# A hybrid conformer and stick-breaking layer: meta scores with the meta keys as the stationary operand, and later, spaced steps for values that are turned and packed

## The chip, the cores and the metric

The kernel runs on one core of a Trainium2 chip. The metric is the device time of one execution in microseconds (us). The engines are TensorE (PE in the profile, with PEld its weight loads), VectorE (DVE), ScalarE (ACT), GpSimd (POOL) and SyncE (SP), which issues DMAs.

## What is computed

One layer over 2048 frames of 1024 channels, with 16 learned meta tokens put ahead of them. All of it is float32.

```python
def hybrid_layer(h, ...):
    u = rms_norm(h, pre_g)
    glu_a, glu_b, conv_gate, q, k, v, sb_gate = split(u @ w_in)      # 7 x 512 columns
    c = causal_depthwise_conv(glu_a * sigmoid(glu_b), conv_w, conv_b)  # width 31
    c = silu(layer_norm(c)) @ w_pw2 + b_pw2
    c = c * silu(conv_gate)
    s = stick_breaking_attention(q, k, v) * silu(sb_gate)            # 8 heads x 64
    return h + rms_norm(concat([c, s]) @ w_out, post_g)

# stick breaking, per head, strictly causal (s < t):
#   z = q.k / 8,  A[t,s] = sigmoid(z[t,s]) * prod over s<j<t of (1 - sigmoid(z[t,j])),  out = A @ v
```

## The kernel before

The frames are worked in four chunks of 512 (`TC`), numbered c = 0 to 3; channels lie on the 128 partitions. A float32 product is made of three products of a high and a low part (`hi`, `lo`, of type fp32r): high by high, high by low, low by high. The projections (`proj`, rows `mm<-uh,w` and `mm<-ul,w`) do so over eight blocks of the contraction; a 128-column block of weights is the stationary operand and 512 frames stream past it.

Attention (`attention`) takes a head and a chunk of keys at a time, in four blocks of 128 queries. `weigh` makes scores into a PSUM bank (`T<-kk,q`), ScalarE takes 1 - sigmoid in place, VectorE's scan multiplies these up from the newest key back (`pr`). `flip` transposes the running products (`T<-ident,pr`) and splits them into `ah` and `al`; `gather` multiplies with the values (`av<-ah,vk`). The running products telescope, so `gather` uses differences of neighbouring values: `differences` makes them on GpSimd (`ev`), and `turn` transposes them by four on TensorE (`T<-ident,ev`), splits them and stores them. `short` lets `gather` go ahead of `weigh` at the last block of a diagonal chunk.

The 16 meta tokens are keys for every query. Their scores are made apart, by `meta_scores`, called for each of the four head pairs j of a chunk 3 us after the pair's query projection: for each block of 128 frames the queries are the stationary operand and the meta keys `km` (32 columns of two heads, high and low) stream past. VectorE adds the two halves into `sgm`, frames on partitions; there are two such tiles, for even and odd chunks, and the second lies in the tile `cp`, so its rows in the profile are named `cp`. When a chunk's attention is done, `meta_keys` turns these scores into weights (a sigmoid, four scans, a copy `bm` on GpSimd), transposes them by four into one PSUM bank, and for each head pair splits 32 rows of that bank into high and low (`mixs<-T,mixs 32x512`) and packs them, high, low and high again, into 96 rows. One product with packed values `vm` (`T<-mixs,vm`) gives the meta tokens' part, to which VectorE adds the attention's sum `sr` and then multiplies with the gate `gt`. The results of all four pairs (`mixs`) are what the output projection `out_proj` of that chunk waits for.

PSUM has eight banks: two for `mm`, four for `T`, one each for `av` and `cv`. `T` banks are taken in a ring: the fourth allocation after one gets the same bank again. The scores of attention, the transposes, the meta scores and the packed products all take `T` banks.

The order of instructions on each engine is set when the program is built. Generators yield the time from which their next piece could run; `merge` chooses between three streams (the attention as main, projections and output as fill, `meta_keys` as extra) by a planner's clock, which has its own costs for each engine's operations (`pe_cost` and others) and corner points (`SHARES`) for how far the fill may be ahead. `when` queues a later step with the tiles it reads and writes. On the chip each engine runs its list in order. All instructions are recorded in one helper, so the profile gives them all line 218; they are told apart by their tiles.

Of the kernel before, what the change touches and what calls it, by code (L numbers as in the profile page):

```python
# [11 lines left out]
F32 = mybir.dt.float32  # L12
F32R = mybir.dt.float32r
# [6 lines left out]
P = 128  # L20
# [3 lines left out]
NM = 16  # L24
# [32 lines left out]
def slab_keys():  # L57
# [17 lines left out]
BEFORE = 0, 2, 0, 0  # L75

SHARES = (
    [(28.1, 169.2)], [(71.5, 214.4)], [(114.3, 214.4)], [(123.8, 97.4), (158.7, 126.3)],
)


# [56 lines left out]
class Later:  # L138
# [1 line left out]

    count = 0

    def __init__(self, clock, what, ins, outs, engine, date, room):
        self.clock, self.what, self.ins, self.outs = clock, what, ins, outs
        self.engine, self.date, self.room = engine, date, room
# [16 lines left out]
    def at(self):  # L162
        t = max([self.date] + [self.clock.at(a, self.n) for a in self.ins])
        if self.room:
            t = max(t, self.clock.next_free(self.room))
        return t


class Engine:
# [51 lines left out]


def pe_cost(name, n, kw):
    return (0.108 if name == "transpose" else max(n * 4.537e-4, 0.06)), 0.19


def dve_cost(name, n, kw):
# [39 lines left out]
def trunk(ctx: ExitStack, tc: tile.TileContext, x, xturn, xlater, meta, cpack, post_g, wpack, out):  # L267
# [13 lines left out]
        while clock.writers(mark):  # L281
            run(clock.writers(mark)[0])

    def when(what, ins, outs=(), engine=None, date=0.0, tag=None):
        soon.append(Later(clock, what, ins, outs, engine, date, tag))

    pe = Engine(clock, nc.tensor, pe_cost, 0.15, run)
    dve = Engine(clock, nc.vector, dve_cost, 0.04, run)
# [42 lines left out]
    def need(*aps, tag=None, given=None, evs=0, n=1):  # L331
# [20 lines left out]
    both = const.tile([P, ncp + NTB * NH * MS], F32, name="cp")  # L352
    cp = both[:, : ncp + KD * NM]
    cw = cp[:, 0 : NJ * CW].rearrange("p (j w) -> p j w", w=CW)
    o = NJ * CW
    preg = cp[:, o : o + KD]
# [26 lines left out]

    vm = const.tile([P, NJ, P], F32R, name="vm")
    vl = const.tile([P, 2, P], F32R, name="vl")
    km = const.tile([P, 2, NJ, 2 * NM], F32R, name="km")
    cm = const.tile([P, NTB, NH, MS], F32, name="cm")
    sgm = [
        const.tile([P, NTB, NH, MS], F32, name="sgm"),
        both[:, ncp:].rearrange("p (b h s) -> p b h s", b=NTB, h=NH),  # L390
    ]
    ct = [const.tile([P, HIST + TC], F32, name=f"ct{j}") for j in range(NJ)]

    def clear():
        for j in range(NJ):
            nc.gpsimd.memset(ct[j][:, 0 : HIST - NM], 0.0)
        nc.gpsimd.memset(km.bitcast(F32), 0.0)
        nc.gpsimd.memset(vm.bitcast(F32), 0.0)
        nc.gpsimd.memset(vl.bitcast(F32), 0.0)
        nc.gpsimd.memset(cm, 0.0)  # L400

    kscr = dr.tile([NH, 2, HD, NM + SEQ], F32, name="kscr")
    qscr = dr.tile([NJ, 2, P, NM + SEQ], F32, name="qscr")
# [494 lines left out]
    def qk_proj(c, g, scr, with_meta):  # L898
        for j in range(NJ):
            o0 = 0 if (with_meta and c == 0) else NM  # L900
            hilo = []

            def ev_qk(pt, o, n):
                if not hilo:
                    hilo.extend(T("ehl", [P, NM + TC], EHL, F32R) for _ in range(2))
                hi, lo = hilo
                act.activation(hi[:, o : o + n], pt, AF.Copy)
                dve.tensor_tensor(
                    lo[:, o : o + n], pt, hi[:, o : o + n].bitcast(F32), op=ALU.subtract
                )  # L910

            yield from proj(c, g + j, ev_qk, with_meta)
            hi, lo = hilo

            def store(j=j, hi=hi, lo=lo):
                cols = slice(c * TC + o0, (c + 1) * TC + NM)
                for i, t in ((0, hi), (1, lo)):
                    if g == G_Q:
                        sp.dma_start(scr[j, i, :, cols], t[:, o0:].bitcast(F32))
                        continue  # L920
                    for e in range(2):
                        sp.dma_start(
                            scr[2 * j + e, i, :, cols],
                            t[e * HD : (e + 1) * HD, o0:].bitcast(F32),
                        )
                if g == G_Q and j == 0:
                    keep["q", c] = True
                    in_us(4.5, lambda: load_first(c))

            when(store, [hi, lo], ["q" if g == G_Q else "k"])  # L930
            if g == G_Q:
                when(
                    lambda a=(c, j, hi, lo): meta_scores(*a), [hi, lo], [sgm[c % 2]], tag="T",
                    date=pe.now + 3.0,
                )

    def meta_scores(c, j, hi, lo):

        sg = sgm[c % 2]
        if j == 0:  # L940
            pool.memset(sg[:, :, :, NM:], 0.0)
        pt = PT("T", [P, TC])[:, : NTB * 4 * NM].rearrange("p (b i s) -> p b i s", b=NTB, i=2)
        for r in range(NTB):
            ts = slice(NM + r * P, NM + (r + 1) * P)
            pe.matmul(pt[:, r], hi[:, ts], km[:, :, j, :], start=(r == 0), stop=False)
            pe.matmul(
                pt[:, r, 0], lo[:, ts], km[:, 0, j, :], start=False, stop=(r == NTB - 1)
            )
        a, b = (pt[:, :, i].rearrange("p b (e s) -> p b e s", e=2) for i in range(2))
        dve.tensor_copy(sg[:, :, 2 * j : 2 * j + 2, 0:NM], b)  # L950
        dve.tensor_tensor(
            sg[:, :, 2 * j : 2 * j + 2, 0:NM], a, sg[:, :, 2 * j : 2 * j + 2, 0:NM], op=ALU.add
        )
        if j == NJ - 1:
            keep["sgm", c] = True

    def in_proj(c):
        yield from pairs(c, range(BEFORE[c], NJ))
# [51 lines left out]
    def values(c):  # L1010
# [3 lines left out]
        for j in range(NJ):  # L1014
# [16 lines left out]
            def differences(vt, j):  # L1031
                o = 0 if c == 0 else NM
                dv = T("ev", [P, 1 + NM + TC], EV)[:, : NM + TC]
                pool.tensor_tensor(
                    dv[:, o:], vt[:, o : NM + TC], vt[:, o + 1 :], op=ALU.subtract
                )
                pool.tensor_copy(vcol[c % 2][:, j], vt[:, NM + P :: P])
                when(lambda: turn(dv, j, P, NM, NTB), [dv], [f"v{j}"], tag="T")
                if c == 0:
                    when(lambda: turn(dv, j, NM, 0, 1), [dv], [f"v{j}"], tag="T")  # L1040

            def turn(dv, j, rows, t0, nb):
                pt = PT("T", [P, NTB, P])[:rows, :nb]
# [26 lines left out]
    def meta_k():  # L1070
        force("k")
        for e in range(2):
            rows = slice(e * HD, (e + 1) * HD)
            for i in range(2):
                sp.dma_start(
                    km[rows, i, :, e * NM : (e + 1) * NM].bitcast(F32),
                    kscr[e::2, i, :, 0:NM].rearrange("j d s -> d j s"),
                )

# [205 lines left out]
    def attention(c, mixs):  # L1285
# [15 lines left out]
        def weigh(u, r):  # L1301
# [22 lines left out]
            u["a"].append(pr)  # L1324
            if kc == 0 and c == NCH - 1 and h >= EARLY:
                bm = keep["bm"][:, h - EARLY, r, h]
                zm = sgm[c % 2][:, r, h, 0:NM]
# [113 lines left out]
        for i in range(len(order) + 1):  # L1441
# [8 lines left out]
                    if 0 < kc == c and h + 1 < NH:  # L1450
                        heads[h + 1] = load_q(c, h + 1)
            for b in range(NTB if u else len(flips)):
                ready = len(pend) >= LAG
                short = ready and pend[0][0]["diag"] and pend[0][1] == NTB - 1
                for what in (1, 0) if short else (0, 1):
                    if what == 0 and u:
                        yield need(heads[u["h"]]["q2"], u["kk"], tag="T")
                        weigh(u, b)
                    if what and ready:
                        yield needs_of(*pend[0])  # L1460
                        gather(*pend.pop(0))
# [41 lines left out]
    def meta_keys(c, h0, h1, mixs):  # L1503
# [10 lines left out]
        hold.add(bm.name)  # L1514
        if part:
            pool.memset(bm, 0.0)
        sg = sgm[c % 2]
        zm = sg[:, :, hs, 0:NM]
        act.activation(zm, zm, AF.Sigmoid, scale=-SCALE)
        for r in range(NTB):  # L1520
            fl = lambda t: t[:, r, hs].rearrange("p h s -> p (h s)")[:, ::-1]
            dve.tensor_tensor_scan(
                fl(sg), fl(sg), fl(cm), 0.0, op0=ALU.mult, op1=ALU.max
            )
        when(lambda: pool.tensor_copy(bm[:, :, hs], zm), [sg], [bm])
        given = {}
        force("s")
        force("g")
# [42 lines left out]
        for j in js:  # L1571
# [347 lines left out]
    def last_room(c):  # L1919
# [8 lines left out]
        zm = sgm[c % 2][:, :, EARLY:, 0:NM]  # L1928
        act.activation(zm, zm, AF.Sigmoid, scale=-SCALE)
        keep["pg"] = a[:, 2:4]  # L1930
        sp.dma_start(
# [109 lines left out]
```

## Time and profile before

| | |
|---|---|
| median of 3 runs | 1317.13 us (1316.32 to 1318.55) |
| the profiled execution | 1318.35 us, its span 1316.6 us |
| TensorE busy | 1292.9 us (98%), 7522 matmuls |
| VectorE busy | 1023.1 us (78%) |
| ScalarE busy | 734.8 us (56%) |
| GpSimd busy | 674.9 us (51%) |
| DMA | 300.82 MB, 228 GB/s on average |

A row of the timeline has the start in us from the span's start, the busy time, the engine, the line, the operation with what it writes and reads, the number of instructions merged and, in brackets, how long the engine stood idle before and who released it. A row of groups has the count, the busy time in us, the mean of one in ns, and the idle time before with its releasers. A row of waits has the total in us, how many times, and the longest. A row of stretches has the length, the busy time of PE, PEld, DVE, ACT and POOL with the number of instructions, the granted TensorE clock as a share of full speed, the DMA share and GB/s. The ends of matmuls are modelled, so the rows of matmuls overlap; their starts are recorded.

### The profile page before, as it was taken

What the parts mean: (1) busy time and instruction counts of PE and PEld (TensorE: products, weight loads), DVE (VectorE), ACT (ScalarE), POOL (GpSimd) and SP (SyncE); (2) the same over time, 40 slices, a digit from 0 to 9 for tenths busy, and PEclk for the clock granted to TensorE, in tenths of its full rate; (3) what the DMA queues carried; (4) which work ended last, traced back from release to release, by engine and by line L of the source; (5) the groups of instructions that cost most, each with busy time, mean ns of one, the idle gap of its engine ahead of it and who ended that gap; (6) DMA issues with size and microseconds to landing.
All of it is one profiled execution on the core that took longest, in us unless ns stands there. A gap on an engine that the chain in (4) does not pass through costs nothing.

```text
span 1316.6 us, 22042 instructions
## 1 busy us (share of the span) xinstructions
PE 1292.9 (98%) x7522; PEld 1115.8 (85%) x7522; DVE 1023.1 (78%) x1470; ACT 734.8 (56%) x1461; POOL 674.9 (51%) x807
## 2 busy tenths in 40 slices
PE   8999999999999999999999999999999999999897
PEld 8998888887799878887789988888787889888797
DVE  5999889998884588984587478985448987899964
ACT  6544355344465452676555544588775665666543
POOL 2555578767677430788742231499787212322402
PEclk9999999999999999999999999999999999999999
DMA  6687787999878996676756696666667456676555
GB/s 230 217 266 234 240 274 258 304 342 321 267 241 269 314 299 196 204 233 215 229 180 193 188 342 198 195 193 215 200 185 231 137 156 191 193 250 217 177 160 184
DMA packets 166399, 300.82 MB, mean 228 GB/s; under 512 B 17280, under 2 KB 71744, under 8 KB 166288
## 3 DMA queue, kind: packets, MB, share of 16 engines
q1 hardware_dynamic: 152496, 251.44, 61.5%
q0 software_dynamic: 13792, 47.98, 9.5%
q8 instruction: 59, 0.97, 0.3%
q14 instruction: 52, 0.43, 0.1%
HBM read 221.90 MB, written 77.46 MB: 227 GB/s over the span
## 4 chain that ended last, share of the span: by engine, by line
PE 86%; DVE 6%; DMA 3%; ACT 2%; issue 1%; POOL 1%; SPq 0%; DVEq 0%; POOLq 0%; ACTq 0%
PE mm L218 56%; PE T L218 21%; PE av L218 9%; DVE pr L218 1%; DMA w<-wscr 1%; DMA ev<-x 1%; DVE ul L218 1%; DVE tok L218 1%; DVE cv L218 1%; DMA tok<-xlater 1%; POOL ev L218 1%; DVE mixs L218 1%; DMA pr<-xturn 0%; DVE al L218 0%; PE cv L218 0%
## 5 line engine op out<-in xcount | busy, mean ns | idle before, releaser
L218 PE MATMUL mm<-uh,w 128*128 128x512 f32 (+1 forms) x1936 | 566.9, 379 | 1.8 <-ACT uh L218 1.5
L218 PEld LDWEIGHTS mm<-uh,w 128*128 128x128 f32 x1936 | 338.7, 190 | 54.2 <-ACT uh L218 2.2
L218 PE MATMUL mm<-ul,w 128*128 128x512 f32 (+1 forms) x968 | 358.9, 372 | 0.0
L218 DVE TENSOR_TENSOR_SCAN pr<-T,pr,zcol 128x512 f32<-128x512 f32 x192 | 245.2, 1277 | 56.6 <-ACT T L218 54.0
L218 DVE TENSOR_TENSOR al<-T,ah 128x512 fp32r<-128x512 f32 (+1 forms) x320 | 191.3, 598 | 102.9 <-ACT ah L218 101.4
L218 ACT ACTIVATE ah<-T 128x512 fp32r<-128x512 f32 (+1 forms) x320 | 170.1, 532 | 156.1 <-PE T L218 155.0
L218 DVE SCALAR_TENSOR_TENSOR cv<-ct,cp,cv 128x512 f32<-128x512 f32 x319 | 238.9, 749 | 6.7
L218 ACT ACTIVATE T<-T 128x512 f32<-128x512 f32 (+2 forms) x320 | 167.5, 525 | 109.6 <-PE T L218 103.8
L218 POOL TENSOR_TENSOR acc<-acc,pd 128x512 f32<-128x512 f32 x150 | 194.7, 1298 | 41.3 <-ACT pd L218 34.6
L218 POOL TENSOR_TENSOR w<-wr,w 128x512 fp32r<-128x512 f32 x132 | 171.3, 1301 | 80.3 <-ACT w L218 79.4
L218 PEld LDWEIGHTS mm<-ul,w 128*128 128x128 f32 x968 | 183.0, 190 | 33.9 <-DVE ul L218 0.7
L218 PE MATMUL T<-kk,q 128*128 128x512 f32 (+3 forms) x640 | 191.8, 383 | 3.4 <-DVE mixs L218 1.1
L218 PE MATMUL T<-ident,pr 128*128 128x128 f32 x1088 | 171.4, 273 | 2.7 <-DVE al L218 1.7
L218 PEld LDWEIGHTS T<-ident,pr 128*128 128x128 f32 x1088 | 135.0, 140 | 35.6 <-DVE al L218 2.7
L218 DVE TENSOR_TENSOR_SCAN pr<-T,tri 128x128 f32<-128x128 f32 (+3 forms) x128 | 103.4, 814 | 28.0 <-ACT T L218 27.8
L218 PEld LDWEIGHTS T<-kk,q 128*128 128x128 f32 x640 | 105.6, 190 | 17.5 <-issue 1.5
L218 PE MATMUL av<-ah,vk 128*128 128x512 f32 (+1 forms) x320 | 119.5, 373 | 0.0
L218 ACT ACTIVATE pd<-ct,cp 128x512 f32<-128x512 f32 x150 | 106.7, 718 | 22.7 <-POOL acc L218 21.9
L218 PE MATMUL av<-al,vk 128*128 128x512 f32 (+1 forms) x320 | 117.2, 366 | 0.0
L218 ACT ACTIVATE w<-wr 128x512 fp32r<-128x512 f32 x140 | 86.9, 626 | 38.5 <-PE mm L218 11.8
L218 POOL COPY cm<-pr 128x1 f32<-128x1 f32 x120 | 23.9, 200 | 135.1 <-DVE pr L218 134.7
L218 PE MATMUL mm<-w,mixc 128*128 128x256 f32 x600 | 80.7, 283 | 0.3 <-ACT tok L218 0.3
(212 smaller groups left out, 1574.8 us busy)
## 6 DMA issues: line engine op xcount, KB each, us to landing
w<-wscr SPq DMA_DIRECT2D x150, 512.0 KB, 4.1
wr<-wpack SPq DMA_DIRECT2D x140, 256.0 KB, 4.5
wscr<-w POOLq DMA_DIRECT2D x68, 512.0 KB, 4.8
kk<-kscr SPq DMA_DIRECT2D x80, 256.0 KB, 4.5
vk<-vscr SPq DMA_DIRECT2D x80, 256.0 KB, 3.8
q<-qscr SPq DMA_DIRECT2D x64, 256.0 KB, 5.5
vscr<-mixs SPq DMA_DIRECT2D x32, 256.0 KB, 3.5
qscr<-ehl SPq DMA_DIRECT2D x32, 256.0 KB, 3.1
```

Source lines behind the costliest of these rows:

```text
L218: return call(out, *args, **kw)
```

## The change

`meta_scores` swaps the sides: the meta keys, in 64 columns, are stationary, and 512 frames of a head pair's queries stream past, first their high part against (low keys, high keys) and then their low part against (high keys, zeros). The result has the scores' two halves on 32 rows each; ScalarE copies one out, VectorE adds the other to it. They gather in a tile `zt` with 32 rows for each pair and frames in columns, which lies in the tile `cp`. At the third step of the chunk's attention four transposes bring it to frames on partitions and one copy fills `sgm`, of which there is now one.

In `meta_keys`, for whole chunks, the four packed steps are kept at least 1.8 us apart on the planner's clock; the sum goes to SBUF rather than back to PSUM, and the product with the gate goes to GpSimd. The value turns are queued 2 us later (`late`). The planner's least cost of a matmul goes from 0.06 to 0.11, `SHARES` is moved by 1.3 to 1.7, and `short` goes.

```diff
-            if g == G_Q:
-                when(lambda a=(c, j, hi, lo): meta_scores(*a), [hi, lo], [sgm[c % 2]], tag="T",
-                    date=pe.now + 3.0)
+            if g == G_Q:
+                when(lambda a=(j, hi, lo): meta_scores(*a), [hi, lo], [zt], tag="T",
+                    date=pe.now + 4.0)
 
-    def meta_scores(c, j, hi, lo):
-        sg = sgm[c % 2]
-        ...
-        for r in range(NTB):
-            ts = slice(NM + r * P, NM + (r + 1) * P)
-            pe.matmul(pt[:, r], hi[:, ts], km[:, :, j, :], start=(r == 0), stop=False)
-            pe.matmul(pt[:, r, 0], lo[:, ts], km[:, 0, j, :], start=False, stop=(r == NTB - 1))
-        dve.tensor_copy(sg[:, :, 2 * j : 2 * j + 2, 0:NM], b)
-        dve.tensor_tensor(sg[:, :, 2 * j : 2 * j + 2, 0:NM], a, sg[...], op=ALU.add)
+    def meta_scores(j, hi, lo):
+        pt = PT("T", [P, TC])
+        for i, t in ((0, hi), (1, lo)):
+            pe.matmul(pt[: 4 * NM], km[:, j, i : i + 2].rearrange("p i s -> p (i s)"), t[:, NM:],
+                start=(i == 0), stop=(i == 1))
+        zj = zt[2 * j * NM : 2 * (j + 1) * NM]
+        act.activation(zj, pt[: 2 * NM], AF.Copy)
+        dve.tensor_tensor(zj, pt[2 * NM : 4 * NM], zj, op=ALU.add)
...
-                when(lambda: turn(dv, j, P, NM, NTB), [dv], [f"v{j}"], tag="T")
+                when(lambda: turn(dv, j, P, NM, NTB), [dv], [f"v{j}"], tag="T", late=2.0)
...
-                ready = len(pend) >= LAG
-                short = ready and pend[0][0]["diag"] and pend[0][1] == NTB - 1
-                for what in (1, 0) if short else (0, 1):
...
+                if u:
+                    yield need(heads[u["h"]]["q2"], u["kk"], tag="T")
+                    weigh(u, b)
+                if len(pend) >= LAG:
+                    yield needs_of(*pend[0])
+                    gather(*pend.pop(0))
...
-            if i == 1:
+            if i == 2:
+                force(zt)
+                yield need(zt, tag="T")
+                pt = PT("T", [P, NTB, NH, NM])
+                for r in range(NTB):
+                    pe.transpose(pt[:, r].rearrange("p h s -> p (h s)"),
+                        zt[:, r * P : (r + 1) * P], ident)
+                dve.tensor_copy(sgm[:, :, :, 0:NM], pt)
+                pool.memset(sgm[:, :, :, NM:], 0.0)
...
-            yield need(m, vm, sr, gt, tag="T")
+            ready, t0 = need(m, vm, sr, gt, tag="T"), pe.now + 1.8
+            yield lambda: ready() if part else max(ready(), t0)
             pj = PT("T", [P, TC])
             pe.matmul(pj, vm[: 6 * NM, j], m[: 6 * NM], start=True, stop=True)
-            dve.tensor_tensor(pj, pj, sr, op=ALU.add)
-            dve.tensor_tensor(sr, pj, gt, op=ALU.mult)
+            dve.tensor_tensor(pj if part else sr, pj, sr, op=ALU.add)
+            (dve if part else pool).tensor_tensor(sr, pj if part else sr, gt, op=ALU.mult)
```

On TensorE, at the first head pair of chunk 0, between two projections (`km` are the meta keys, `ehl` the queries' parts), there stood before:

```order
L218 MATMUL mm<-ul,w 128x512
L218 MATMUL T<-km,ehl 128x64
L218 MATMUL T<-km,ehl 128x32
L218 MATMUL T<-km,ehl 128x64
L218 MATMUL T<-km,ehl 128x32
L218 MATMUL T<-km,ehl 128x64
L218 MATMUL T<-km,ehl 128x32
L218 MATMUL T<-km,ehl 128x64
L218 MATMUL T<-km,ehl 128x32
L218 MATMUL mm<-uh,w 128x512 x2
```

and there stand now

```order
L218 MATMUL mm<-ul,w 128x512
L218 MATMUL T<-ehl,km 64x512 x2
L218 MATMUL mm<-uh,w 128x512 x2
L218 MATMUL mm<-ul,w 128x512
L218 MATMUL mm<-uh,w 128x512 x2
```

Eight matmuls of 64 and 32 columns became two of 512.

On TensorE, in chunk 3, where the meta values of chunk 2 are packed (`vm` are the packed values, `T<-ident,pr` a flip of the attention), the second packed product and what follows it were before:

```order
L218 MATMUL mm<-ul,w 128x512
L218 MATMUL T<-mixs,vm 128x512
L218 MATMUL T<-ident,pr 128x128 x2
L218 MATMUL mm<-uh,w 128x512 x2
L218 MATMUL mm<-ul,w 128x512
```

Now the first packed product has that place (the fourth allocation of a `T` bank after the transposed weights), and behind it stand

```order
L218 MATMUL T<-mixs,vm 128x512
L218 MATMUL mm<-uh,w 128x512 x2
L218 MATMUL mm<-ul,w 128x512
L218 MATMUL mm<-uh,w 128x512 x2
L218 MATMUL mm<-ul,w 128x512
L218 MATMUL T<-kk,q_11175 128x512 x2
L218 MATMUL T<-ident,pr 128x128 x2
L218 MATMUL T<-kk,q_11175 128x512 x2
```

The flip has moved behind six matmuls of a projection.

On VectorE, in chunk 1, ahead of the four splits of the packed weights (`mixs<-T,mixs`; `cv` is a tap of the convolution), there stood before:

```order
L218 SCALAR_TENSOR_TENSOR pr<-T,tri 128x384
L218 COPY cp<-T 128x4x2x16
L218 TENSOR_TENSOR cp<-T,cp 128x4x2x16
L218 SCALAR_TENSOR_TENSOR cv<-ct_95,cp,cv 128x512 x2
L218 SCALAR_TENSOR_TENSOR pr<-T,tri 128x512
L218 TENSOR_TENSOR mixs<-T,mixs 32x512 x4
```

and now

```order
L218 SCALAR_TENSOR_TENSOR pr<-T,tri 128x384
L218 SCALAR_TENSOR_TENSOR pr<-T,tri 128x512
L218 TENSOR_TENSOR cp<-T,cp 32x512
L218 SCALAR_TENSOR_TENSOR cv<-ct_95,cp,cv 128x512
L218 TENSOR_TENSOR mixs<-T,mixs 32x512 x4
```

The scores' add now stands behind the last scan, next to the splits.

More of the change, by code (lines that the diff above doesn't have):

```diff
@@ L77 @@
 SHARES = (
-    [(28.1, 169.2)], [(71.5, 214.4)], [(114.3, 214.4)], [(123.8, 97.4), (158.7, 126.3)],
+    [(29.8, 169.2)], [(73.1, 214.4)], [(116.0, 214.4)], [(125.1, 97.4), (160.4, 126.3)],
 )
@@ L141, with __init__ @@
     count = 0
-    def __init__(self, clock, what, ins, outs, engine, date, room):
+    def __init__(self, clock, what, ins, outs, engine, date, room, late):
         self.clock, self.what, self.ins, self.outs = clock, what, ins, outs
-        self.engine, self.date, self.room = engine, date, room
+        self.engine, self.date, self.room, self.late = engine, date, room, late
         Later.count += 1
@@ L165, in at @@
             t = max(t, self.clock.next_free(self.room))
-        return t
+        return t + self.late
 class Engine:
@@ L223, in pe_cost @@
 def pe_cost(name, n, kw):
-    return (0.108 if name == "transpose" else max(n * 4.537e-4, 0.06)), 0.19
+    return (0.108 if name == "transpose" else max(n * 4.537e-4, 0.11)), 0.19
 def dve_cost(name, n, kw):
@@ L282, in force, with when @@
             run(clock.writers(mark)[0])
-    def when(what, ins, outs=(), engine=None, date=0.0, tag=None):
-        soon.append(Later(clock, what, ins, outs, engine, date, tag))
+    def when(what, ins, outs=(), engine=None, date=0.0, tag=None, late=0.0):
+        soon.append(Later(clock, what, ins, outs, engine, date, tag, late))
     pe = Engine(clock, nc.tensor, pe_cost, 0.15, run)
@@ L351, in trunk @@
     ncp = NJ * CW + KD + 4 * NJ
-    both = const.tile([P, ncp + NTB * NH * MS], F32, name="cp")
-    cp = both[:, : ncp + KD * NM]
+    both = const.tile([P, ncp + TC], F32, name="cp")
+    cp, zt = both[:, : ncp + KD * NM], both[:, ncp:]
     cw = cp[:, 0 : NJ * CW].rearrange("p (j w) -> p j w", w=CW)
@@ L385, in trunk @@
     vl = const.tile([P, 2, P], F32R, name="vl")
-    km = const.tile([P, 2, NJ, 2 * NM], F32R, name="km")
+    km = const.tile([P, NJ, 3, 2 * NM], F32R, name="km")
     cm = const.tile([P, NTB, NH, MS], F32, name="cm")
[L388 to L391, printed above, removed]
+    sgm = const.tile([P, NTB, NH, MS], F32, name="sgm")
     ct = [const.tile([P, HIST + TC], F32, name=f"ct{j}") for j in range(NJ)]
@@ L400, in clear @@
         nc.gpsimd.memset(cm, 0.0)
+        nc.gpsimd.memset(sgm, 0.0)
     kscr = dr.tile([NH, 2, HD, NM + SEQ], F32, name="kscr")
@@ L932, in qk_proj @@
                 when(
-                    lambda a=(c, j, hi, lo): meta_scores(*a), [hi, lo], [sgm[c % 2]], tag="T",
-                    date=pe.now + 3.0,
-                )
-    def meta_scores(c, j, hi, lo):
-        sg = sgm[c % 2]
-        if j == 0:
-            pool.memset(sg[:, :, :, NM:], 0.0)
-        pt = PT("T", [P, TC])[:, : NTB * 4 * NM].rearrange("p (b i s) -> p b i s", b=NTB, i=2)
-        for r in range(NTB):
-            ts = slice(NM + r * P, NM + (r + 1) * P)
-            pe.matmul(pt[:, r], hi[:, ts], km[:, :, j, :], start=(r == 0), stop=False)
+                    lambda a=(j, hi, lo): meta_scores(*a), [hi, lo], [zt], tag="T",
+                    date=pe.now + 4.0,
+                )
+    def meta_scores(j, hi, lo):
+        pt = PT("T", [P, TC])
+        for i, t in ((0, hi), (1, lo)):
             pe.matmul(
-                pt[:, r, 0], lo[:, ts], km[:, 0, j, :], start=False, stop=(r == NTB - 1)
-            )
-        a, b = (pt[:, :, i].rearrange("p b (e s) -> p b e s", e=2) for i in range(2))
-        dve.tensor_copy(sg[:, :, 2 * j : 2 * j + 2, 0:NM], b)
[L951 to L955, printed above, removed]
+                pt[: 4 * NM], km[:, j, i : i + 2].rearrange("p i s -> p (i s)"), t[:, NM:],
+                start=(i == 0), stop=(i == 1),
+            )
+        zj = zt[2 * j * NM : 2 * (j + 1) * NM]
+        act.activation(zj, pt[: 2 * NM], AF.Copy)
+        dve.tensor_tensor(zj, pt[2 * NM : 4 * NM], zj, op=ALU.add)
     def in_proj(c):
@@ L1037, in differences @@
                 pool.tensor_copy(vcol[c % 2][:, j], vt[:, NM + P :: P])
-                when(lambda: turn(dv, j, P, NM, NTB), [dv], [f"v{j}"], tag="T")
+                when(lambda: turn(dv, j, P, NM, NTB), [dv], [f"v{j}"], tag="T", late=2.0)
                 if c == 0:
-                    when(lambda: turn(dv, j, NM, 0, 1), [dv], [f"v{j}"], tag="T")
+                    when(lambda: turn(dv, j, NM, 0, 1), [dv], [f"v{j}"], tag="T", late=2.0)
             def turn(dv, j, rows, t0, nb):
@@ L1075, in meta_k @@
                 sp.dma_start(
-                    km[rows, i, :, e * NM : (e + 1) * NM].bitcast(F32),
+                    km[rows, :, 1 - i, e * NM : (e + 1) * NM].bitcast(F32),
                     kscr[e::2, i, :, 0:NM].rearrange("j d s -> d j s"),
@@ L1326, in weigh @@
                 bm = keep["bm"][:, h - EARLY, r, h]
-                zm = sgm[c % 2][:, r, h, 0:NM]
+                zm = sgm[:, r, h, 0:NM]
                 when(
@@ L1452, in attention @@
             for b in range(NTB if u else len(flips)):
-                ready = len(pend) >= LAG
-                short = ready and pend[0][0]["diag"] and pend[0][1] == NTB - 1
-                for what in (1, 0) if short else (0, 1):
[L1456 to L1461, printed above, removed]
+                if u:
[4 more added lines that the diff above has]
+                    gather(*pend.pop(0))
                 if u and b == NTB - 1:
@@ L1474, in attention @@
                 load_first(c + 1)
-            if i == 1:
+            if i == 2:
[3 more added lines that the diff above has]
+                for r in range(NTB):
+                    pe.transpose(
+                        pt[:, r].rearrange("p h s -> p (h s)"), zt[:, r * P : (r + 1) * P], ident
+                    )
+                dve.tensor_copy(sgm[:, :, :, 0:NM], pt)
+                pool.memset(sgm[:, :, :, NM:], 0.0)
+                keep["sgm", c] = True
                 if c == 0:
@@ L1516, in meta_keys @@
             pool.memset(bm, 0.0)
-        sg = sgm[c % 2]
-        zm = sg[:, :, hs, 0:NM]
+        zm = sgm[:, :, hs, 0:NM]
         act.activation(zm, zm, AF.Sigmoid, scale=-SCALE)
@@ L1522, in meta_keys @@
             dve.tensor_tensor_scan(
-                fl(sg), fl(sg), fl(cm), 0.0, op0=ALU.mult, op1=ALU.max
+                fl(sgm), fl(sgm), fl(cm), 0.0, op0=ALU.mult, op1=ALU.max
             )
-        when(lambda: pool.tensor_copy(bm[:, :, hs], zm), [sg], [bm])
+        when(lambda: pool.tensor_copy(bm[:, :, hs], zm), [sgm], [bm])
         given = {}
@@ L1927, in last_room @@
         pool.memset(a[:, 4:6], 0.0)
-        zm = sgm[c % 2][:, :, EARLY:, 0:NM]
+        zm = sgm[:, :, EARLY:, 0:NM]
         act.activation(zm, zm, AF.Sigmoid, scale=-SCALE)
```

## The prediction

> **What bounds the kernel now.** I read the page's totals and its chain of waits first, then TensorE's own waits, then the timeline at the places that the change touches.
>
> ```profile
> span 1316.6 us, 22042 instructions
> PE 1292.9 (98%) x7522; PEld 1115.8 (85%) x7522; DVE 1023.1 (78%) x1470; ACT 734.8 (56%) x1461; POOL 674.9 (51%) x807
> PE 86%; DVE 6%; DMA 3%; ACT 2%; issue 1%; POOL 1%; SPq 0%; DVEq 0%; POOLq 0%; ACTq 0%
> ```
>
> TensorE is the bound: it is busy for 98% of the span and 86% of the last chain runs over it. So an instruction taken from TensorE is worth its whole time, and work added elsewhere costs only where TensorE comes to wait for it. Its named waits are small:
>
> ```profile
> PE T L218 <- DVE mixs L218: 3.7, 3, 1.7
> PE T L218 <- POOL ev L218: 2.2, 3, 1.3
> PE T L218 <- DVE pr L218: 2.0, 4, 1.0
> PE T L218 <- DVE al L218: 1.7, 3, 1.1
> ```
>
> The first row is the packed meta values (`meta_keys`), the second the value turns (`turn`); the change touches both. The last two belong to the attention's rhythm.
>
> **The meta scores on TensorE.** One of the 16 groups (four chunks, four head pairs):
>
> ```profile
> 119.12 0.96 PE L218 MATMUL T<-km,ehl 128*128 128x64 f32 x8
> 119.93 0.71 PE L218 MATMUL mm<-uh,w 128*128 128x512 f32 x2
> 120.48 0.39 PE L218 MATMUL mm<-ul,w 128*128 128x512 f32 x1
> 120.71 0.63 PE L218 MATMUL mm<-uh,w 128*128 128x512 f32 x2
> ```
>
> Matmul ends are modelled, so I go by starts. A 512-wide matmul holds TensorE for 0.23 us (120.48 to 120.71). From 119.12 to 120.48, 1.36 us, stand the eight score matmuls and two such matmuls (0.46): a group costs 0.90 us, the load of eight different 128-column blocks, not the 64 or 32 columns that stream past them. Sixteen groups: 14.4 us. After, a group is two 512-wide matmuls, 0.46 us, 7.4 us in all. New are four groups of four transposes at the attention's third step; their price comes from four others:
>
> ```profile
> 994.09 0.60 PE L218 MATMUL T<-ident,ev 128*128 128x128 f32 x4
> 994.44 0.71 PE L218 MATMUL mm<-uh,w 128*128 128x512 f32 x2
> 994.99 0.39 PE L218 MATMUL mm<-ul,w 128*128 128x512 f32 x1
> ```
>
> 994.09 to 994.99 is 0.90, less 0.46: 0.44 us a group, 1.8 us in all. Term A: 7.4 + 1.8 - 14.4 = -5.2 us, all on the path.
>
> No matmul with 64 stationary columns and 512 moving ones is in the trace. The nearest row has five transposes, of which the fifth loads 16 columns:
>
> ```profile
> 93.11 0.77 PE L218 MATMUL T<-ident,ev 128*128 128x128 f32 x5
> 93.63 0.49 PE L218 MATMUL mm<-uh,w 128*128 128x264 f32 x2
> 93.96 0.29 PE L218 MATMUL mm<-ul,w 128*128 128x264 f32 x1
> ```
>
> 93.11 to 93.63 is 0.52 for five, 0.10 each: a narrow stationary block neither empties nor delays the array here. If it did, the bound would be one matmul's tail, the 0.39 that a row is long less the 0.23 until the next starts, 0.16, at each end of each pair: 32 x 0.16 = 5.1 us. I take zero and keep 5.1 as a rival. [...]
>
> **The same edit on the other engines.**
>
> ```profile
> L218 DVE COPY sgm<-T 128x128 f32<-128x128 f32 x8 | 2.3, 287 | 7.2 <-PE T L218 7.2
> L218 DVE TENSOR_TENSOR sgm<-T,sgm 128x128 f32<-128x128 f32 x8 | 2.3, 292 | 0.3
> L218 DVE TENSOR_TENSOR mixs<-T,mixs 32x512 fp32r<-32x512 f32 x12 | 8.2, 685 | 6.0 <-ACT mixs L218 5.9
> L218 ACT ACTIVATE mixs<-T 32x512 fp32r<-32x512 f32 x12 | 7.1, 590 | 10.3 <-DVE mixs L218 9.2 <-PE T L218 1.1
> L218 DVE TENSOR_TENSOR tok<-T,tok 128x512 f32<-128x512 f32 x12 | 8.3, 691 | 0.4
> L218 POOL TENSOR_TENSOR tok<-tok,ev 128x512 f32<-128x512 f32 x24 | 30.9, 1288 | 67.9 <-DMA ev<-post_g 49.8 <-ACT tok L218 14.0 <-ACT ah L218 4.0
> ```
>
> VectorE loses 16 x (0.287 + 0.292) = 9.3 us, gains 16 adds of 0.685 and four wide copies at about as much (13.7), and hands 12 products of 0.691 (8.3) to GpSimd: -3.9 us. ScalarE gains 16 copies of 0.59 (9.4 us), GpSimd 12 products at 1.288 (15.5 us). At 78, 56 and 51% busy this lies beside TensorE; if that cover goes, the price is the rival below. What counts is how long a group holds its `T` bank: copy and add one after the other, 1.28 us, where two short reads took 0.58. Between 0 and 1.3 us in all (once, where the bank is next asked for while others are held), I take +0.6 us, term E, since only the three places with packed values have full banks.
>
> **The later value turns.** The longest of the three waits:
>
> ```profile
> 599.30 0.62 PE L218 MATMUL T<-kk,q 128*128 128x512 f32 x2
> 600.08 1.04 POOL L218 TENSOR_TENSOR ev<-ev 128x512 f32<-128x512 f32 x1
> 601.17 0.66 PE L218 MATMUL T<-ident,ev 128*128 128x128 f32 x4 [1.25 <-POOL ev L218]
> ```
>
> The turn is placed before GpSimd has made the differences. Two microseconds more exceed the longest wait (1.25), and the order does move the turns: ahead of this one (chunk 2's third block) now stand 446 of the wide `mm<-ul` matmuls instead of 442, ahead of chunk 1's fourth 230 instead of 226. Between 0 and a little over 2.2 us: I take all, with what the modelled tails hide: term B, -2.5 us. The stores leave some 2 us later; the query projection stands between them and their first reader, so nothing is late next.
>
> **The packed values in spaced steps.** Chunk 3's place:
>
> ```profile
> 999.49 0.40 PE L218 MATMUL mm<-ul,w 128*128 128x512 f32 x1
> 1000.78 0.69 DVE L218 TENSOR_TENSOR mixs<-T,mixs 32x512 fp32r<-32x512 f32 x1 [0.66 <-ACT mixs L218]
> 1001.62 0.47 PE L218 MATMUL T<-mixs,vm 96*128 96x512 f32 x1 [1.73 <-DVE mixs L218]
> 1002.56 0.44 PE L218 MATMUL T<-ident,pr 128*128 128x128 f32 x2 [0.47 <-DVE al L218]
> 1003.53 0.94 PE L218 MATMUL mm<-uh,w 128*128 128x512 f32 x2
> 1006.40 0.94 PE L218 MATMUL mm<-uh,w 128*128 128x512 f32 x2
> 1007.18 0.39 PE L218 MATMUL mm<-ul,w 128*128 128x512 f32 x1
> 1003.50:1006.90 3.40, 3.40 (x10) 2.58 (x9) 3.33 (x7) 0.84 (x2) 3.40 (x4) 0.52 0.20 77
> ```
>
> The second packed product waits until 1001.47 (1000.78 + 0.69), when VectorE has read the last of the four splits out of the bank of the transposed weights: it is the fourth bank taken after that bank, and there are four. A second wait follows, and then a stretch at a granted clock of 0.52: nine matmuls from 1003.53 to 1007.18, 3.65 us where nine take 2.09, so 1.56 lost. In the new order the fourth bank is again asked for about as early, now by the first packed product, and splits are made as before; so I leave the 1.73 us in place. But a piece of projection stands behind it instead of the transposes: the second wait goes (0.47), and with 1.7 idle instead of 2.2 I expect the clock to hold (waits of 1.25 and 1.14, alone, did not lower it). Term C: -2.0 us; bounds 0 and -4. [...]
>
> Chunk 1 has the same chain:
>
> ```profile
> 352.06 0.39 PE L218 MATMUL mm<-ul,w 128*128 128x512 f32 x1
> 352.75 0.69 DVE L218 TENSOR_TENSOR mixs<-T,mixs 32x512 fp32r<-32x512 f32 x1 [0.66 <-ACT mixs L218]
> 353.59 0.70 PE L218 MATMUL T<-kk,q 128*128 128x512 f32 x2 [1.14 <-DVE mixs L218]
> ```
>
> There the score's new add comes right ahead of the splits on VectorE, 0.685 with a tap behind it, where the short pair was done earlier: about 1 us later, at an unchanged place of TensorE. Term D: +1.0 us; bounds 0 and +2.5, the latter if the longer wait also lowers the clock.
>
> The dropped swap of gather and weigh and the planner's new cost (0.11) only move work that stays: bounds -2 and +2 us, about the `DVE al` or `DVE pr` row; I take zero.
>
> **Sum.** -5.2 - 2.5 - 2.0 + 1.0 + 0.6 = -8.1 us on the profiled execution's 1318.35 (1316.6 span and 1.8 around it): 1310.2. The median of the three runs, 1317.13, is 1.2 lower, which gives 1309.0. A measurement tells about 0.2%, 2.6 us, from no change (the runs lie 2.2 apart).
>
> **Rivals.**
> - *Only the scores pay* (0.20): waits B and C stay or move elsewhere in the new plan; 1317.1 - 5.2 + 1.6 = 1313.5. For it: every wait comes from a plan that mistakes durations, and a new plan makes new mistakes. Against: the turns really stand later.
> - *All goes well* (0.16): the chain of splits comes early enough in all three chunks (another 1.1 + 0.9 + 1.7 by the first wait row's 3.7), and the clock holds in the tail too (as at chunk 3, 1.6): 1309.0 - 5.3 = 1303.7. Against: the splits still alternate between two engines.
> - *The narrow block drains the array* (0.04): 1309.0 + 5.1 = 1314.1; with the waits not cured, no change. Against: the 16-column row.
> - *No change within 0.2%* (0.10): as the first rival, and the new plan adds waits as long as the last two wait rows (3.7) once more: about 1317.
> - *Slower* (0.06): the products on GpSimd. Each of the four steps of a chunk now has 1.29 us there ahead of the last split, 5.2 us a chunk, behind the weights' splits. Nothing else can start the output projection, so if GpSimd's backlog passes the attention work that TensorE has left to do until then, two chunks would cost 10.3: 1319.3. Against: it is 51% busy, and in the new order 40 wide matmuls at 0.23 us and 49 short ones at about 0.11 (0.44 / 4), 14.6 us, stand between chunk 1's last packed product and the output projection.
>
> **How the numbers follow.** The forecast, 1306 to 1312, holds 0.44. Faster by over 0.2% (below 1314.5): 0.44 + 0.20 + 0.16 and half of the drain's 0.04, 0.82. Within: 0.10 and the other 0.02, 0.12. Slower: 0.06. The range 1303.0 to 1316.5 leaves out the slower case, a part of no change and the best of the good one.
>
> **What would show it.** TensorE has 7442 matmuls; the score group two, 0.46 us from start to start, with the next matmul 0.23 after; the row of waits for `POOL ev` nearly gone; the wait for `DVE mixs` still at 3 or more; no stretch at half clock near 1000 us. I am wrong if the score pair takes over 0.6 us, if `PE T <- POOL` grows, or if the waits in the attention's tail (from 1230 us on) grow.

## The result and the profile after

| | before | after |
|---|---|---|
| median, us | 1316.99 (1316.32 to 1318.55, 4 runs) | 1309.83 (1306.39 to 1310.56, 4 runs) |
| ratio, 95% interval | | 0.9939 (0.9919 to 0.9958) |
| profiled execution, span | 1318.35, 1316.6 | 1310.08, 1308.3 |

The kernel became 0.6% faster. The forecast was 1309.0 within 1303.0 to 1316.5, and faster with 0.82. The total came out within 1 us; the way to it did not, and the experiments show why that matters.

The page's totals and the last chain of the kernel after:

```profile
span 1308.3 us, 21884 instructions
PE 1284.2 (98%) x7442; PEld 1106.2 (85%) x7442; DVE 1019.9 (78%) x1446; ACT 743.3 (57%) x1477; POOL 691.5 (53%) x820
PE 84%; DVE 6%; DMA 4%; issue 2%; ACT 2%; POOL 1%; SPq 0%; DVEq 0%; POOLq 0%; ACTq 0%
```

TensorE is still the bound. The other engines moved as forecast: VectorE -3.2 us (forecast -3.9), ScalarE +8.5 (9.4), GpSimd +16.6 (15.5), all beside TensorE. TensorE's own waits (total, times, longest, in us), without four rows that are as long as before (`POOL ident` 1.8, `ACT uh` 1.5, `DVE ul` 1.2, `DVE ehl` 0.9) and those under 0.4:

```profile
PE T L218 <- DVE pr L218: 4.4, 6, 1.0
PE T L218 <- DVE mixs L218: 4.2, 3, 2.5
PE T L218 <- DVE al L218: 1.1, 1, 1.1
PE av L218 <- POOL rate L218: 0.9, 1, 0.9
```

The row of waits for `POOL ev` (2.2 before) is gone. The row `DVE mixs` has grown from 3.7 to 4.2, and `DVE pr` from 2.0 to 4.4.

The score pair and what surrounds it, from the timeline, and the four kinds of work that the change added, from the groups:

```profile
117.95 0.39 PE L218 MATMUL mm<-ul,w 128*128 128x512 f32 x1
118.18 0.63 PE L218 MATMUL T<-ehl,km 128*64 128x512 f32 x2
118.64 0.63 PE L218 MATMUL mm<-uh,w 128*128 128x512 f32 x2
119.11 0.39 PE L218 MATMUL mm<-ul,w 128*128 128x512 f32 x1
L218 DVE TENSOR_TENSOR cp<-T,cp 32x512 f32<-32x512 f32 x16 | 11.0, 685 | 8.0 <-ACT cp L218 7.7
L218 ACT ACTIVATE cp<-T 32x512 f32<-32x512 f32 x16 | 9.4, 587 | 17.9 <-PE T L218 17.9
L218 POOL TENSOR_TENSOR tok<-tok 128x512 f32<-128x512 f32 x12 | 15.5, 1296 | 0.7 <-DVE tok L218 0.6 <-PE T L218 0.2
L218 DVE COPY sgm<-T 128x512 f32<-128x512 f32 x4 | 2.7, 674 | 0.0
```

The pair takes 0.46 us (118.18 to 118.64), the matmul ahead of it 0.23, and the two behind it 0.47: no sign of a drain.

To say where the 8 us went I measured every distance between the starts of two successive matmuls and took off the distance of an unhindered matmul of that width (0.4537 ns a moving column, at least 0.109 us; the medians in the trace of before are 0.233 us for 512 columns, 0.108 for 128 and 0.112 for 64 and for 32). What is left over, the *excess*, holds waits and half-clock stretches. The rows of single places add up only distances of over 0.12 us too much; what is smaller falls into the last row. Over the whole trace:

| us | before | after | difference |
|---|---|---|---|
| unhindered matmuls | 1271.4 | 1266.6 | -4.8 |
| excess, all | 36.4 | 32.7 | -3.7 |
| of it: value turns | 3.4 | 0 | -3.4 |
| chunk 1's splits and scores | 1.3 | 3.0 | +1.7 |
| chunk 2's | 2.2 | 1.9 | -0.3 |
| chunk 3's, with the half clock | 4.0 | 4.2 | +0.2 |
| all other places together | 25.5 | 23.6 | -1.9 |

Chunk 3's place in the kernel after, TensorE with the first and the last of the four splits on VectorE, and the stretch behind it:

```profile
986.13 0.68 DVE L218 TENSOR_TENSOR mixs<-T,mixs 32x512 fp32r<-32x512 f32 x1
988.09 0.40 PE L218 MATMUL mm<-ul,w 128*128 128x512 f32 x1
990.15 0.69 DVE L218 TENSOR_TENSOR mixs<-T,mixs 32x512 fp32r<-32x512 f32 x1 [0.66 <-ACT mixs L218]
990.99 0.47 PE L218 MATMUL T<-mixs,vm 96*128 96x512 f32 x1 [2.50 <-DVE mixs L218]
991.20:994.90 3.70, 3.70 (x12) 2.87 (x11) 2.60 (x4) 1.97 (x6) 3.68 (x5) 0.54 0.16 22
```

The wait is 2.50 us where it was 1.73, and the clock still falls (0.54 over that stretch). Before, the first split there stood at

```profile
996.76 0.68 DVE L218 TENSOR_TENSOR mixs<-T,mixs 32x512 fp32r<-32x512 f32 x1
```

Chunk 1's place in the kernel after:

```profile
340.48 0.68 PE L218 MATMUL T<-ehl,km 128*64 128x512 f32 x2 [0.83 <-DVE pr L218]
341.20 0.59 ACT L218 ACTIVATE cp<-T 32x512 f32<-32x512 f32 x1 [0.93 <-PE T L218]
343.00 0.69 DVE L218 TENSOR_TENSOR cp<-T,cp 32x512 f32<-32x512 f32 x1
343.02 0.59 ACT L218 ACTIVATE mixs<-T 32x512 fp32r<-32x512 f32 x1 [1.24 <-PE T L218]
343.72 0.75 DVE L218 SCALAR_TENSOR_TENSOR cv<-ct,cp,cv 128x512 f32<-128x512 f32 x1
344.51 0.68 DVE L218 TENSOR_TENSOR mixs<-T,mixs 32x512 fp32r<-32x512 f32 x1
348.15 0.39 PE L218 MATMUL mm<-ul,w 128*128 128x512 f32 x1
348.52 0.69 DVE L218 TENSOR_TENSOR mixs<-T,mixs 32x512 fp32r<-32x512 f32 x1 [0.66 <-ACT mixs L218]
349.36 0.47 PE L218 MATMUL T<-mixs,vm 96*128 96x512 f32 x1 [0.82 <-DVE mixs L218]
350.58 0.73 PE L218 MATMUL T<-kk,q 128*128 128x512 f32 x2 [0.76 <-DVE pr L218]
```

The score's add (343.00) and a tap (343.72) stand ahead of VectorE's first split, which starts 0.90 us after ScalarE's half of it was ready (343.61). Before, the first split was no earlier: behind two taps and a scan it started 1.03 us after ScalarE's half (347.71):

```profile
347.12 0.59 ACT L218 ACTIVATE mixs<-T 32x512 fp32r<-32x512 f32 x1
348.74 0.68 DVE L218 TENSOR_TENSOR mixs<-T,mixs 32x512 fp32r<-32x512 f32 x1
```

### The profile page after: what moved, and what is told of

It is laid out like the page before. It is cut to its first block, busy times and chain, and to the rows that moved or that the text cites. A ratio compares the mean times of both kernels' runs of the same rounds, so it can differ in the third digit from the quotient of the medians.

```text
span 1308.3 us, 21884 instructions
## 1 busy us (share of the span) xinstructions
PE 1284.2 (98%) x7442; PEld 1106.2 (85%) x7442; DVE 1019.9 (78%) x1446; ACT 743.3 (57%) x1477; POOL 691.5 (53%) x820
## 4 chain that ended last, share of the span: by engine, by line
PE 84%; DVE 6%; DMA 4%; issue 2%; ACT 2%; POOL 1%; SPq 0%; DVEq 0%; POOLq 0%; ACTq 0%
PE mm L218 55%; PE T L218 19%; PE av L218 9%; DVE pr L218 2%; DMA wr<-wpack 1%; DVE ul L218 1%; DVE tok L218 1%; DMA ev<-x 1%; DMA tok<-x 1%; DMA w<-wscr 1%; DMA tok<-xlater 1%; DVE sgm L218 1%; DVE mixs L218 0%; ACT ev L218 0%; PE cv L218 0%
## 5 line engine op out<-in xcount | busy, mean ns | idle before, releaser
L218 POOL TENSOR_TENSOR ev<-ev 64x512 f32<-64x512 f32 (+2 forms) x46 | 55.5, 1207 | 67.4 <-ACT ev L218 39.0
```

Source lines behind the costliest of these rows:

```text
L218: return call(out, *args, **kw)
```

## The experiments

My first theory was the prediction's own: each edit is worth what it takes off TensorE's path, and the terms add. Its rival: the edits only pay together, or the order that the planner happens to make decides as much as the edits do.

### The parts alone

**The new meta scores alone**, in the kernel before (old `SHARES`, cost, swap, turns and packed steps):

```diff
-            pe.matmul(pt[:, r], hi[:, ts], km[:, :, j, :], start=(r == 0), stop=False)
...
+            pe.matmul(
+                pt[: 4 * NM], km[:, j, i : i + 2].rearrange("p i s -> p (i s)"), t[:, NM:],
+                start=(i == 0), stop=(i == 1),
+            )
...
```

> The meta scores alone are changed; turns, packed steps, planner's cost and the swap are as before. If TensorE's work carries the gain (16 groups from 0.90 to 0.46 us, four groups of transposes at 0.44): 5.2 us less than before, 1311 to 1313, with the waits for POOL ev (2.2 us) and for DVE mixs (3.7) still there. If the gain came mainly from the waits that the other edits remove: under 3 us less, above 1314. If the whole gain is the scores': 1309.

Measured: 1318.91 us (1316.02 to 1320.35, 10 runs) against 1316.86; ratio 1.0008 (0.9997 to 1.0020). No gain. The unhindered matmuls fell by the same 4.8 us, but the excess rose from 36.4 to 42.0. The longest of the new waits is at a place that the edit does not touch, in the attention:

```profile
208.34 0.39 PE L218 MATMUL mm<-ul,w 128*128 128x512 f32 x1
210.96 0.44 PE L218 MATMUL T<-kk,q 128*128 128x128 f32 x2 [2.24 <-DVE pr L218]
PE T L218 <- DVE pr L218: 6.7, 8, 2.2
```

**All but the scores**, the complement; against the change:

```diff
-        zj = zt[2 * j * NM : 2 * (j + 1) * NM]
-        act.activation(zj, pt[: 2 * NM], AF.Copy)
-        dve.tensor_tensor(zj, pt[2 * NM : 4 * NM], zj, op=ALU.add)
+        a, b = (pt[:, :, i].rearrange("p b (e s) -> p b e s", e=2) for i in range(2))
+        dve.tensor_copy(sg[:, :, 2 * j : 2 * j + 2, 0:NM], b)
...
```

> All edits but the meta scores, which stay as eight matmuls a group. If the gains add: the rest is worth the 7.2 us of the whole less the scores' 5.2, so 2 to 3 us less than before, 1314 to 1315, with no wait for POOL ev. If the rest does nothing by itself: 1317.

Measured: 1318.82 us (1317.54 to 1323.67, 10 runs); ratio 1.0014 (1.0002 to 1.0026). No gain either. The waits for `POOL ev` are gone here too; others came: 2.9 us at 193 to 198 (`DVE ul`), 1.4 at 493, 1.1 at 428. (The traced execution, the fastest of the ten, has an excess of 35.8 us, little under the 36.4 before.) So neither half pays, and both together pay 8 us. The terms do not simply add.

**The change without the later value turns:**

```diff
-  when(lambda: turn(dv, j, P, NM, NTB), [dv], [f"v{j}"], tag="T", late=2.0)
+  when(lambda: turn(dv, j, P, NM, NTB), [dv], [f"v{j}"], tag="T")
```

> The changed kernel with the value turns queued as before (no 2 us more). If the turns' waits are worth what the trace of before showed: TensorE waits for POOL ev again, 2 to 3.5 us in all, and the time is 2 to 3.5 us above the changed kernel's, 1312 to 1313. If GpSimd has the differences in time in the new plan anyway: no such wait and the changed kernel's time.

Measured: 1318.47 us (1315.85 to 1319.77, 10 runs); ratio 1.0009 (0.9999 to 1.0020), 8.6 us above the change. The waits at the turns are back, five of them, 4.1 us of starts:

```profile
610.64 0.66 PE L218 MATMUL T<-ident,ev 128*128 128x128 f32 x4 [1.21 <-POOL ev L218]
PE T L218 <- POOL ev L218: 3.3, 5, 1.2
```

Most of the rest is chunk 1, whose excess is 5.9 us here (3.0 in the change), 1.6 of it a stretch at half clock, and 1.3 at 702 and 722. These places have no value turn, so I put them down to the new order; that is argued, not tested.

**The change without the spacing of the packed steps** and with sum and product back on VectorE:

```diff
-            ready, t0 = need(m, vm, sr, gt, tag="T"), pe.now + 1.8
-            yield lambda: ready() if part else max(ready(), t0)
+            yield need(m, vm, sr, gt, tag="T")
...
-            dve.tensor_tensor(pj if part else sr, pj, sr, op=ALU.add)
-            (dve if part else pool).tensor_tensor(sr, pj if part else sr, gt, op=ALU.mult)
+            dve.tensor_tensor(pj, pj, sr, op=ALU.add)
+            dve.tensor_tensor(sr, pj, gt, op=ALU.mult)
```

> The changed kernel with the packed steps unspaced and sum and product back on VectorE in PSUM. The trace of the changed kernel has the long wait for DVE mixs at the first packed product, ahead of any spacing. If the spacing does nothing for it: the same wait for DVE mixs (4.2 us, longest 2.5), the half clock after it, and a time within 1.5 us of the changed kernel's. If the spacing and GpSimd's product are needed: waits for DVE tok or T behind the first step, and 2 to 5 us more.

Measured: 1310.24 us (1308.02 to 1311.09, 4 runs); ratio 0.9940 (0.9922 to 0.9958), the change's own time. The wait in chunk 3 is the same to the hundredth:

```profile
991.64 0.47 PE L218 MATMUL T<-mixs,vm 96*128 96x512 f32 x1 [2.50 <-DVE mixs L218]
```

So the spaced steps and GpSimd's products bring nothing and cost nothing that these runs can tell.

**Scores and later turns** in the kernel before, with its old cost, `SHARES`, swap and packed steps; against the kernel with the new scores alone:

```diff
-                when(lambda: turn(dv, j, P, NM, NTB), [dv], [f"v{j}"], tag="T")
+                when(lambda: turn(dv, j, P, NM, NTB), [dv], [f"v{j}"], tag="T", late=2.0)
```

> Before, with the new meta scores and the value turns queued 2 us later, and nothing else (old planner cost and corner points, old swap, old packed steps). The scores alone gave no gain, the changed kernel without the later turns none either. If these two together make the gain: 1309 to 1311. If the planner's cost or the swap is needed too: 1314 to 1318. If the differences between such kernels are mostly what a new plan does to waits here and there, anything between.

Measured: 1324.03 us (1322.71 to 1325.80, 4 runs); ratio 1.0062 (1.0047 to 1.0077), slower, with the two edits in it that the prediction valued most. One wait in chunk 1, with half clock from 346.36 to 353.19, explains most; a wait at 501 us, again with half clock, adds to it:

```profile
348.30 1.19 PE L218 MATMUL T<-kk,q 128*128 128x512 f32 x2 [4.61 <-DVE mixs L218]
348.40:351.80 3.40, 3.40 (x8) 2.57 (x9) 2.55 (x3) 2.27 (x5) 3.40 (x3) 0.50 0.97 305
```

### Does the order alone move the time?

**The kernel before, and the kernel after, with every corner point of `SHARES` 1 us later.** Nothing is computed otherwise; the planner only decides a few things differently.

```diff
-    [(28.1, 169.2)], [(71.5, 214.4)], [(114.3, 214.4)], [(123.8, 97.4), (158.7, 126.3)],
+    [(29.1, 169.2)], [(72.5, 214.4)], [(115.3, 214.4)], [(124.8, 97.4), (159.7, 126.3)],
```

> Before, with the planner's corner points moved by 1.0 and no other edit: the same instructions in a slightly other order. If a plan alone moves the time by several us through waits: 1313 to 1322, and the single effects above are to be read with that much play. If plans are stable: within 1.5 us of before.

> The changed kernel with its corner points moved by another 1.0. If the gain is of the edits: within 2 us of the changed kernel, 1308 to 1312. If it is a lucky plan: 1312 to 1318.

Measured: before nudged 1323.28 us (1322.31 to 1325.21, 4 runs), ratio to before 1.0057 (1.0042 to 1.0072); after nudged 1313.03 (1309.87 to 1314.70, 10 runs), ratio to before 0.9971 (0.9962 to 0.9981). So an order alone is worth +6.6 us in the one kernel and +3.2 in the other (4.2 by the ratios), as much as most of the edits. The unhindered time is unchanged in both. Before nudged has waits of 2.1 and 1.5 us (`DVE ct`) that the kernel before has not; its excess is 40.8 where that was 36.4. After nudged was traced in the fastest of its ten runs (1309.87), with the excess of the change (32.9), so where the other runs lost their 3 us was not seen. Either way the changed kernel is the faster: by 7 us as they stand, by 10 with both nudged.

### The same order, with TensorE's work changed

These two take the planner out: matmuls are added or left out behind its back, so that every engine's order stands word for word.

**The change with two more 512-wide matmuls in each score group** (a block of zeros that is added):

```diff
+            if i == 0:
+                for _ in range(2):
+                    nc.tensor.matmul(pt[: 2 * NM], km[:, j, 2], hi[:, NM:], start=False, stop=False)
```

> The changed kernel with two more 512-wide matmuls in each of the 16 score groups, a block of zeros (32 columns) against the queries' high parts; put past the planner, so that every engine's order stands as in the changed kernel. 32 x 0.23 = 7.4 us more on TensorE. Theory (TensorE's time counts whole when the order is held; what moved the time in the nudged kernels was the order): +6.5 to +8, about 1317. Rival (the waits take up such time whatever the order, so the scores' 5.2 us were never worth 5.2): +0 to +4, 1310 to 1314. Second rival (the narrow block drains the array after all): +12 or more.

Measured: 1314.67 us (1313.17 to 1317.76, 11 runs), 4.8 above the change; ratio to before 0.9982 (0.9972 to 0.9992), which is 0.0043 or 5.7 us above the change's ratio, uncertain by some 2.9. This lies between the two forecasts. In the traced executions the difference is 3.4 us, and they show where the rest of the 7.4 went: the excess fell by 4.0 us, 1.1 of it in chunk 1 and 2.0 in chunk 3, where TensorE comes later to the same chain of splits and the clock holds this time:

```profile
995.57 0.47 PE L218 MATMUL T<-mixs,vm 96*128 96x512 f32 x1 [2.03 <-DVE mixs L218]
995.80:999.40 3.60, 3.60 (x18) 2.88 (x18) 3.36 (x6) 2.86 (x8) 3.58 (x5) 1.00 0.16 23
```

**The kernel before without the 64 score matmuls of the queries' low parts:**

```diff
-            return call(out, *args, **kw)
+            return None if skip else call(out, *args, **kw)
...
-                pt[:, r, 0], lo[:, ts], km[:, 0, j, :], start=False, stop=(r == NTB - 1)
+                pt[:, r, 0], lo[:, ts], km[:, 0, j, :], start=False, stop=False, skip=True
```

> The kernel before without the 64 score matmuls of 32 moving columns (the queries' low parts are left out of the meta scores); the planner still counts them, so that every engine's order stands as before. By 0.90 us for eight they take 0.11 each, 7.2 us in all. Theory: -6 to -7.5, about 1310. Rival (waits grow where TensorE has less to do): -0 to -4, 1313 to 1317.

Measured: 1311.77 us (1308.91 to 1312.80, 5 runs) against 1317.15; ratio 0.9951 (0.9937 to 0.9965), 6.5 us less (4.6 to 8.3). The profiled span fell by 6.6 us, the unhindered matmuls by 7.0, and the excess rose by 0.5. With the order held, TensorE's time counted nearly whole when it was taken away (6.6 us of span for 7.0); when it was added, shorter waits made up for part of it (4.0 of 7.4). The rival theory stands in this form: an edit's time on TensorE is real, and on top of it every new order draws new waits: where the excess was 36.4 before, it lay between 30.3 and 46.1 us in the kernels with new orders. Which of the planner's cost, the corner points and the dropped swap gives the changed kernel its good order was not run apart and stays open.

### The bank of the transposed weights

**The change with one ScalarE copy of the transposed weights to SBUF in whole chunks**, from which the splits are made, so that the bank is free sooner:

```diff
+        if not part:
+            out = ev()[:, :TC]
+            act.activation(out, pt, AF.Copy)
+            pt = out
```

> The changed kernel, with one ScalarE copy that brings the transposed weights from the T bank into SBUF, from where the four splits read. If the bank held by four alternating splits is what TensorE waits for (DVE mixs, 4.2 us, and 1.5 at half clock behind the longest): these waits go, and 4 to 6 us, to 1304 to 1306, less what the new plan adds. If the splits' lateness itself holds the first packed product: the wait stays under another name and the time is the changed kernel's.

> The changed kernel with the transposed weights copied out of their PSUM bank by one ScalarE copy, as once before (1307.9), beside two kernels that hold their order. If the 2 us under the changed kernel are the waits for the bank that went (1.0 + 0.7 + 2.5 us), it comes again at 1306 to 1309; if it was the spread of the runs, 1309 to 1311.

Measured: 1307.87 us (1307.65 to 1308.37, 4 runs), ratio 0.9940 (0.9923 to 0.9956); again 1309.05 (1307.81 to 1310.73, 5 runs), ratio 0.9937 (0.9925 to 0.9950). By the ratios no different from the change (0.9939). The 4.2 us of waits for `DVE mixs` are gone, but TensorE now waits for VectorE's other work at those places. Of the first run:

```profile
PE T L218 <- DVE pr L218: 4.5, 8, 1.0
PE T L218 <- DVE al L218: 3.2, 3, 1.3
```

Of the 4.2 us, 2.1 came back as `DVE al` (3.2 here, 1.1 in the change). So the bank was part of the wait and a late VectorE the rest; in all the excess fell to 30.3 and 31.0 us from 32.7, which is less than the ratios can tell. No version that I ran is measurably faster than the change.

## Why the prediction was right, and where it was not

- **A, the scores, -5.2: right.** 7442 matmuls; the pair 0.46 us, no drain; unhindered time -4.8. That such time reaches the end when the order is held is shown where it was taken away, 6.5 of 7.0 us; where it was added, some 5 of 7.4 came through, with an uncertainty of 2.9. The rival of a drain is out: behind 29 of the 32 such matmuls the next starts 0.22 to 0.24 us later, as behind their neighbours, and behind the other three, which follow a wait or a flip, 0.28 to 0.32. At these plain blocks of 64 columns between blocks of 128 the trace shows no drain.
- **B, the value turns, -2.5: right, and too small.** 3.4 us of starts went at the turns: I had counted only the waits as the list names them (2.2), with a little for the tails. Without the edit 4.1 came back.
- **C, the packed values, -2.0: wrong; it was +0.2.** The step that failed is "the fourth bank is again asked for about as early". Counted from the start of VectorE's first split, the last one ends 4.71 us later in both kernels. TensorE asked for the bank 2.96 us after that start before (999.72, which is 0.23 after the start of the last projection, from 996.76) and asks 2.19 after it now (988.32 from 986.13): 0.77 sooner, and the wait grew by just that, 1.73 to 2.50. The second wait (0.47) did go. The clock did not hold (0.54 behind the wait): I had expected 1.7 us idle, and it was 2.5. That the edit in the code does nothing there is shown by the kernel without it.
- **D and E, +1.0 and +0.6: near in their sum, by luck; the mechanism of D was wrong.** D has VectorE's splits later by the score's add and the wait for them longer. But before, the first split was already 1.03 us late, now 0.90, and the wait shrank, 1.14 to 0.82: the last split ends 4.70 us after the start of the first in both kernels, and TensorE asks 3.87 us after that start (348.38 from 344.51) where it asked 3.55 after it (352.29 from 348.74), 0.32 later. Chunk 1's excess still grew by 1.7, by two waits for `DVE pr` that neither term names: of its 3.0 us now, 1.0 is ahead of the score pair (340.48), 1.0 the splits', 1.0 the attention behind them (350.58).
- **"Only move work that stays: bounds -2 and +2": the step most wrong, though the sum hid it.** Two nudges of the plan moved the time by +6.6 and +3.2 us with no work changed, and the kernels with parts of the change drew as much. In the change as it stands all other places came out at -1.9, which with the surplus of B (0.9) made good what C lost (2.2). So the total was right partly by luck; the sign was less so, since it also held with both plans nudged.
- **The rivals.** "Only the scores pay" had the right reason, that a new plan makes new mistakes, but the turns paid too. GpSimd's products, the slower case, cost nothing: with and without them the time is the same.
- The tail (from 1230 us before, 1222 after) did not grow: an excess of 6.0 before, 5.7 after.

## What to carry to other kernels

In a kernel whose order is planned, an edit is measured together with a new order, and the order may weigh as much as the edit: here 3 to 7 us of 1317 against a change of 8. Run a nudge of the plan that changes no work before crediting or rejecting a part; to price an instruction, add or drop it behind the planner's back so that the order stands. When a buffer names a long wait, look at which engine is late before freeing the buffer: here the wait was the time at which the last split was done less the time at which TensorE asked for the bank, and copying the bank out gained nothing measurable.

## What the runs showed of the hardware

In these traces the length of a wait alone did not set whether the clock fell to half. The bank-free kernel, run twice, has the same two waits in chunk 3 in both traces, yet the stretch behind them ran at a granted clock of 0.50 in the first and 1.00 in the second:

```profile
990.44 0.47 PE L218 MATMUL T<-mixs,vm 96*128 96x512 f32 x1 [0.85 <-DVE al L218]
991.54 0.44 PE L218 MATMUL T<-ident,pr 128*128 128x128 f32 x2 [0.63 <-DVE pr L218]
988.89:992.30 3.41, 1.93 (x8) 0.91 (x7) 3.38 (x5) 1.41 (x3) 3.39 (x5) 1.00 0.31 91
992.30:995.71 3.41, 3.41 (x9) 2.64 (x8) 3.41 (x5) 0.68 (x2) 3.41 (x4) 0.50 0.51 147
```

```profile
992.68 0.47 PE L218 MATMUL T<-mixs,vm 96*128 96x512 f32 x1 [0.86 <-DVE al L218]
993.79 0.44 PE L218 MATMUL T<-ident,pr 128*128 128x128 f32 x2 [0.63 <-DVE pr L218]
989.70:993.12 3.42, 2.56 (x11) 1.57 (x9) 3.30 (x4) 2.49 (x5) 3.34 (x4) 1.00 0.60 182
993.12:996.53 3.41, 2.77 (x13) 2.10 (x13) 3.41 (x6) 0.97 (x2) 3.39 (x4) 1.00 0.55 154
```

The change without later turns waited 2.46 us for the first packed product and kept its clock (1.00 behind the wait), while the change waited 2.50 and did not (0.54):

```profile
1000.94 0.47 PE L218 MATMUL T<-mixs,vm 96*128 96x512 f32 x1 [2.46 <-DVE mixs L218]
1001.20:1004.80 3.60, 3.60 (x18) 2.89 (x18) 3.37 (x6) 2.88 (x7) 3.58 (x5) 1.00 0.10 28
```

Each trace records when the granted clock changed. In each of the 13 traces these changes are whole multiples of 3.41333 us apart, to 0.003 us: in the change the two halved stretches begin at 991.53 and 1227.05, 69 such steps apart. A halved stretch lasted one step (two in a row in one kernel, 346.36 to 353.19). In the traces of before and of the change the four at chunk 3 and in the tail hold 1.4 to 1.6 us of excess each; 512-wide matmuls start 0.427 us apart in them, where the median of the whole trace of before is 0.233.

I then added up, step by step on this grid, how long TensorE stood idle by the starts of its matmuls, from the first grant of the full clock to the last matmuls. All 22 falls to half clock in that range come right behind a step with 1.96 to 2.98 us idle, and none of the 4876 other steps at full clock has more than 2.02. In the trace of before the three falls stand behind 2.22 to 2.37 us, and no other step has more than 1.40; in the change the two stand behind 2.40 and 2.73, and no other has more than 1.92. In the first run of the bank-free kernel both waits lie in one step (2.18 us idle); in the second the boundary at 993.12 parts them (1.22 and 1.00). The kernel without later turns has a boundary at 1000.01, within its wait (1.78 and 1.00); the change has its whole wait in one step (2.73). This is what 13 traces show side by side; no run moved a boundary on purpose, so that the idle time of a step is the cause was not shown.

For this kernel, then, a forecast would ask how much idle time can fall into one such step. Behind a step with less than 1.96 us idle the clock stayed in every trace. If that holds, a single wait of 2.5 us leaves the clock alone only where a boundary leaves less than 2.0 on either side, which for a boundary at a random place is, as an estimate from these figures, 1.5 in 3.41 or 0.44.
